# Two-layer mLSTM and convolution trunk: the sums of squares of x issued first, and gated products and gates in another order

## Chip, cores and metric

One Trainium2 chip, one of its cores. The metric is the device time of one launch in microseconds (us). The kernel before took 1609.53 us, the median of three runs (1607.35 to 1611.52).

## What is computed

A trunk of two layers over 512 tokens of 1024 features, all in float32, steered by a vector c. Cut to what matters here:

```python
for l in range(2):
    mod = silu(c) @ w_ada[l] + b_ada[l]            # six rows of 1024: shift, scale, gate, twice
    h = rms_norm(x, g_pre_mix) * (1 + sc_mix) + sh_mix
    x_m, z, glu_a, glu_b = split(h @ w_in[l])      # 4 x 1024 columns
    x_c = silu(causal_conv4(x_m))
    q, k, v = per head of 256: x_c @ w_q, x_c @ w_k, x_m @ w_v
    gates = [q k v] @ w_gates + b_gates            # input and forget gate, 4 heads each
    h_m = sigmoid(z) * head_norm(mlstm(q, k, v, gates))
    a = silu(group_norm(causal_conv31(glu_a * sigmoid(glu_b))))   # 8 groups of 128 channels
    y = concat(h_m, a) @ w_out[l]
    x = x + gt_mix * rms_norm(y, g_post_mix)
    x = x + gt_mlp * rms_norm(relu(h2 @ w_ff1)**2 @ w_ff2, g_post_mlp)   # h2 from x as h above
```

The conv of 31 taps is depthwise: each channel of the gated product has its own 31 weights.

## The kernel before

**Layout.** x lies transposed as eight tiles of 128 features x 512 tokens. A projection of 1024 inputs onto 128 outputs ("a block") is 24 matmuls of 512 columns: weights and h are each split into a high and a low part, and three products are summed (`passes`, L177 to L179). Weights come in by DMA into one of four `raw` buffers; ScalarE rounds the high part (L169), GpSimd, or at the start VectorE, subtracts the low one (L170).

**The mixer.** A string in `ORDERS` (L66) names the order in which the steps of a mixer are emitted. `X i` makes two blocks of x_m, `V i` the conv of four taps with silu, `Q i` q, k and v of head i, the transposes of v (L567) and the head's share of the gates, which VectorE adds up in `gsb` (L578, L583). `G i` makes gated product i out of two blocks (`glu`, L441; VectorE's product is L438). `E` is the gates: two matmuls on `gsb` (L591, L592), a chain of short operations on four partitions that goes between ScalarE and VectorE (L596 to L622) and ends in `mm` (L622), then TensorE's transposes of `al` (L625) and of `mm` (L626) and the tables that VectorE makes of them (L636, L640). `Z i` is a block of the output gate. `N i` is a strip of c's product in layer 0 (L245 to L258). `a i` are the scores of head i: a matmul that spreads `ml` (L647), VectorE's sum (L652), the score products (L660), and VectorE's product (L662), which frees the bank of `mm`-tagged PSUM that L660 filled; there are three such banks. `b`, `c` are the rest of a head, `C i` the 31-tap convs of two groups and their norms, `O` the output projection. The products G0 to G2 are made ahead of the string.

**The convs.** All eight convs of a layer run on VectorE: 31 rows of 128 x 512 a group (the first is L427, the others L429), 248 rows a layer. They are emitted late in the string, with the lowest priority. After each one comes `conv_norm` (L474): ScalarE copies the result (L476), TensorE transposes it (L479), VectorE takes mean and variance (L485, L486, L146) and normalises (L490), TensorE transposes back (L494), VectorE multiplies (L500).

**What sets the order of work.** Each engine has one queue and works through it in order; an instruction that waits holds all that stand behind it. The queues are made before the launch: a list scheduler takes the instructions by priority in a time model of its own and puts conv rows where it reckons that VectorE is free. `behind(later, earlier)` fixes an order of issue, and no wait between engines.

**The start.** DMA issues stand in SyncE's queue. ScalarE and VectorE make silu of c for all partitions (`silu(cbc)`, L210 to L212), then eight squares (L809) and seven sums (L811) of x. TensorE adds over the features (L814), VectorE and GpSimd make the root (L815, L816), TensorE spreads it (L819), and for each tile VectorE and ScalarE make h (L351, L357, L358). TensorE begins with six blocks of layer 0 at once, one tile of h after the other, each with its weights in a `raw` of 384 KB (L168).

Of the kernel before, what the change touches and what calls it, by code (L numbers as in the profile page):

```python
# [10 lines left out]
F32 = mybir.dt.float32  # L11
F32R = mybir.dt.float32r
AF = mybir.ActivationFunctionType
ALU = mybir.AluOpType
PSUM = bass.MemoryType.PSUM

P = 128
T = 512
D = 1024
# [3 lines left out]
NF = D // P  # L23
NC = T // P
KDW = 31
EPS = 1e-6
# [27 lines left out]
def trunk(ctx, tc, xT, vecs, bg, cst, ccol, crow, wadn, wadt, win, win0, wqkv, wgate, wout, wff1, wff2, yT):  # L54
    nc = tc.nc
    pe, dve, act, pool, sp = nc.tensor, nc.vector, nc.scalar, nc.gpsimd, nc.sync
# [3 lines left out]
    wpool = ctx.enter_context(tc.tile_pool(name="wpool", bufs=1))  # L60
    scr = ctx.enter_context(tc.tile_pool(name="scr", bufs=1))
# [1 line left out]
    ps = ctx.enter_context(tc.tile_pool(name="ps", bufs=1, space=PSUM))  # L63

    NSLOT = 25
    ORDERS = ['X0 G3 V0 X1 Q0 V1 N4 G4 X2 G5 N5 Q1 V2 X3 N6 Q2 V3 G6 Q3 E G7 N7 Z0 Z1 Z2 Z3 N8 a0 Z4 b0 Z5 a1 b1 Z6 N9 c0 C0 a2 Z7 c1 b2 C1 C2 C3 O0 O1 a3 O2 c2 O6 O3 b3 O4 O5 c3 O7', 'X0 V0 G3 X1 Q0 V1 X2 G4 Q1 V2 G5 X3 Q2 V3 G7 Q3 E Z0 G6 Z1 Z2 Z3 a0 Z4 Z5 b0 a1 Z6 b1 Z7 c0 a2 c1 C0 b2 C1 C2 C3 O0 O1 a3 O6 O2 c2 O3 b3 O4 O5 c3 O7']  # L66
    WPRI = 300
    NK = 4
    KM = 4
# [4 lines left out]
    RAW = 4  # L74
# [6 lines left out]
    BPRI = 4000  # L81
# [7 lines left out]
    def slot(shape=(P, 2, T), dt=F32):  # L89
        return slots.tile(list(shape), dt, name="slot", tag="slot", bufs=NSLOT)  # L90

    def s2(shape=(P, T), dt=F32):
        return scr.tile(list(shape), dt, name="s2", tag="s2", bufs=S2)
# [4 lines left out]
    def small(n, tag="sm", bufs=16, dt=F32):  # L98
        return sm.tile([P, n], dt, name="small", tag=tag, bufs=bufs)

    def bank(tag, shape=(P, T)):
        n = {"mm": 3, "cv": 2, "ax": 2, "cx": 1}[tag]
        return ps.tile(list(shape), F32, name="ps_" + tag, tag=tag, bufs=n)

    def behind(later, earlier):
        tc.add_manual_dep(later.ins, earlier.ins.name, mybir.DependencyInfo(mybir.DependencyClass.NoSync,
                          mybir.DependencyReason.DATA), reason="order of issue")
# [6 lines left out]
    def r32(ap):  # L114
        return ap.bitcast(F32R)
# [4 lines left out]
    cbc = slots.tile([P, 2, T], F32, name="cbc", tag="slot", bufs=NSLOT).rearrange("p a b -> p (a b)")  # L120
    x = [keep.tile([P, T], F32, name=f"x{i}") for i in range(NF)]
    cc = keep.tile([P, NF], F32, name="cc")
# [10 lines left out]
    ones = cs[:, C_ONE:C_ONE + P]  # L133

    def vec(name, l):
        o, w = VOFF[name]
        return vv[:, l, o:o + w]

    mhalf = keep.tile([P, NC], F32, name="mhalf")
# [10 lines left out]
    def split(pair, src, hi_eng=None, lo_eng=None):  # L150
# [4 lines left out]
            act.copy(out=hi, in_=src)  # L155
        (lo_eng or dve).tensor_tensor(lo, src, pair[:, 0, :], op=ALU.subtract)

    def wblock(src, alloc=None, lo_eng=None, pri=None):
        n = src.shape[-1]
        with tc.high_priority(offset=WPRI if pri is None else pri):  # L160
            flat = lambda t: t.rearrange("p a b -> p (a b)")
            raw = wpool.tile([P, n], F32, name="raw", tag="raw", bufs=RAW)
            if alloc is not None:
                hi, lo = flat(alloc())[:, 0:n], flat(alloc())[:, 0:n]
            else:
                hi = wpool.tile([P, n], F32, name="whi", tag="whi", bufs=WHI)
                lo = wpool.tile([P, n], F32, name="wlo", tag="wlo", bufs=WLO)
            sp.dma_start(out=raw, in_=src)  # L168
            act.copy(out=r32(hi), in_=raw)  # L169
            (lo_eng or pool).tensor_tensor(r32(lo), raw, hi, op=ALU.subtract)  # L170
        return hi, lo

    def passes(out, w, col, pair, first, last, ts=slice(0, T)):
# [9 lines left out]
    def gemm(blocks, pairs):  # L183
        out = bank("mm")
        for b, src in enumerate(blocks):
            spare[0] -= 1
            w = wblock(src, ytile if spare[0] >= 0 else None)
            for k in range(8):
                passes(out, w, k * P, pairs[b * 8 + k], b == 0 and k == 0, b == len(blocks) - 1 and k == 7)
        return out  # L190
# [15 lines left out]
    def half(hf):  # L206
        return slice(hf * (T // 2), (hf + 1) * (T // 2))

    def silu(t, th):
        act.activation(out=th, in_=t, func=AF.Tanh, scale=0.5)  # L210
        act.activation(out=t, in_=t, func=AF.Copy, scale=0.5)
        dve.scalar_tensor_tensor(t, th, 1.0, t, op0=ALU.add, op1=ALU.mult)  # L212

    silu(cbc, wpool.tile([P, D], F32, name="raw", tag="raw", bufs=RAW))
    silu(cc, small(NF))

    hgb = keep.tile([P, L, 24], F32, name="hgb")

# [1 line left out]
    mods = [keep.tile([P, 48], F32, name=f"mod{l}") for l in range(L)]  # L220
    inits = [keep.tile([P, 48], F32, name=f"ini{l}") for l in range(L)]

    def prepare(l):
        for q, (one, gain) in enumerate(ADA):
            k = slice(8 * q, 8 * q + 8)
            if gain is None:
                dve.tensor_copy(out=inits[l][:, k], in_=vec("b_ada", l)[:, k])
            else:
                dve.scalar_tensor_tensor(inits[l][:, k], vec("b_ada", l)[:, k], one, vec(gain, l),
                                         op0=ALU.add, op1=ALU.mult)  # L230

    def ada_rows(nb, tag, alloc=None):

# [28 lines left out]
    def ada_col(l, c, alloc=None):  # L262

        one, gain = ADA[c // 8]
        scale = 1.0 if gain is None else vec(gain, l)[:, c % 8:c % 8 + 1]
        if alloc is not None:
            raw = alloc().rearrange("p a b -> p (a b)")
        else:
            raw = wpool.tile([P, D], F32, name="adr", tag="adr", bufs=ADR)
        sp.dma_start(out=raw, in_=wadt[l, c])  # L270
        m, ini = mods[l][:, c:c + 1], inits[l][:, c:c + 1]
        red = dve.tensor_tensor_reduce(raw, raw, cbc, scale, 0.0 if one else ini, ALU.mult, ALU.add, m)  # L272
        if last[0] is not None:
            behind(red, last[0])
        if one and alloc is not None:
            dve.tensor_tensor(m, m, ini, op=ALU.add)
        elif one:
            late.append((l, c))
# [67 lines left out]
    def make_h(l, i, src, bc, ts, pr, a_off, sh_off, tmp=None):  # L346

        sh = mods[l][:, sh_off + i:sh_off + i + 1]
        hpool = i in HPOOL and ts.stop - ts.start < T
        t = s2() if tmp is None or hpool else tmp(i)  # L350
        dve.scalar_tensor_tensor(t[:, ts], src, mods[l][:, a_off + i:a_off + i + 1], bc, op0=ALU.mult, op1=ALU.mult)  # L351
        if hpool:
            act.activation(out=t[:, ts], in_=t[:, ts], func=AF.Identity, bias=sh)
            act.copy(out=r32(pr[:, 0, ts]), in_=t[:, ts])
            pool.tensor_tensor(r32(pr[:, 1, ts]), t[:, ts], pr[:, 0, ts], op=ALU.subtract)  # L355
            return
        act.activation(out=r32(pr[:, 0, ts]), in_=t[:, ts], func=AF.Identity, bias=sh)  # L357
        dve.scalar_tensor_tensor(r32(pr[:, 1, ts]), t[:, ts], sh, pr[:, 0, ts], op0=ALU.add, op1=ALU.subtract)  # L358

    def finish(l, which, blocks, pairs, y, allocs, nxt):  # L360

# [53 lines left out]
    def mixer(l, hp, pre):  # L415
# [309 lines left out]
        hm = []  # L725
        for step in ORDERS[l].split():
            i = int(step[1:] or 0)
# [74 lines left out]
        return finish(l, "mlp", [wff2[l, 1, m, 1] for m in range(NF)], fp[8:], y, [slot] * KF,  # L802
                      (mix_start(l + 1), [slot] * MK) if l + 1 < L else None)

    prepare(0)
    ss0 = scr.tile([P, T], F32, name="rl", tag="rl", bufs=3)
    for i in range(NF):
        sq = ss0 if i == 0 else scr.tile([P, T], F32, name="rl", tag="rl", bufs=3)
        act.activation(out=sq, in_=x[i], func=AF.Square)  # L809
        if i:  # L810
            dve.tensor_tensor(ss0, ss0, sq, op=ALU.add)  # L811
    v0, u0, r0 = bank("ax"), small(NC), small(NC)
    for c in range(NC):
        pe.matmul(v0[:, c:c + 1], ss0[:, c * P:(c + 1) * P], ones[:, 0:1], start=True, stop=True)  # L814
    dve.tensor_scalar(u0, v0[:, 0:NC], 1.0 / D, EPS, op0=ALU.mult, op1=ALU.add)  # L815
    pool.tensor_tensor(r0, u0, mhalf, op=ALU.pow)  # L816
    bc0 = bank("ax")
    for c in range(NC):
        pe.matmul(bc0[:, c * P:(c + 1) * P], r0[:, c:c + 1].broadcast_to([P, P]), ident, start=True, stop=True)  # L819
    hp, pre = [], {}  # L820
    for j in range(NF // 2):
        if j > 1:
            ada_rows(j, "ax", slot if j == 2 else None)
        for i in (2 * j, 2 * j + 1):
            if j < 2:
                ada_col(0, i, slot)
                ada_col(0, 8 + i, slot)
            pre[i] = wblock(win0[i], slot, dve, 0)
            hp.append(slot())
            make_h(0, i, x[i], bc0, slice(0, T), hp[i], 8, 0)  # L830
    sp.dma_start(out=bgt, in_=bg)
    for l in range(L):
        dve.tensor_scalar(hgb[:, l, 0:8], vec("g_cn", l), 0.5, None, op0=ALU.mult)
        dve.tensor_scalar(hgb[:, l, 8:16], vec("b_cn", l), 0.5, None, op0=ALU.mult)
        dve.tensor_scalar(hgb[:, l, 16:24], vec("b_dw", l), 2.0, None, op0=ALU.mult)
    prepare(1)
    for l in range(L):
        hp, pre = mixer(l, hp, pre)
        hp, pre = mlp(l, hp, pre)
# [61 lines left out]
```

## Time and profile before

| what | value |
|---|---|
| median of three runs | 1609.53 us |
| the profiled execution | 1608.05 us |
| its span, first to last instruction | 1606.3 us |
| busy share of TensorE / VectorE / GpSimd / ScalarE | 96% / 55% / 50% / 43% |
| rows of conv on VectorE | 480 (L429) and 16 (L427) |
| bytes moved | 188.91 MB, mean 118 GB/s |

The program's time is that of the profiled execution, 1.75 us over its span. Busy shares are means over the span; matmuls are pipelined, so a busy TensorE is not one at its peak. The mixer of layer 0 lies between about 70 and 400 us, that of layer 1 between about 860 and 1180 us; between and behind them are the MLPs.

### The profile page before, as it was taken

To read this page: it belongs to the slowest core of one execution; us is meant where nothing else is said; L and a number is where in the kernel's file an instruction comes from. 1 tells how busy PE (TensorE), PEld (TensorE's weight loads), DVE (VectorE), ACT (ScalarE), POOL (GpSimd) and SP (SyncE) were. 2 spreads that over 40 slices of the span, in tenths; PEclk is the share of its full clock that TensorE was granted. 3 is DMA by queue.
4 is the path that set the end of the run, shared out by engine and by line. 5 is a ranking of instruction groups with operands and counts; after the bars stand their busy time and mean duration, and the time that the engine had idled before them with its cause. 6 is when DMAs were issued, how large, how long until landed. Compare 5 with 4: busy or idle time off the path is not lost.

```text
span 1606.3 us, 21229 instructions
## 1 busy us (share of the span) xinstructions
PE 1537.6 (96%) x8020; PEld 1255.5 (78%) x8020; DVE 878.1 (55%) x1761; ACT 688.6 (43%) x1168; POOL 798.5 (50%) x488
## 2 busy tenths in 40 slices
PE   4899998999999999999999999999999999999997
PEld 3577665677998888888899777676899888888887
DVE  6399999843164432346747999997326320012114
ACT  3345563453454322332453665544355432233242
POOL 0166662256744444445962877434674444444462
PEclk9999999999999999999999999999999999999999
DMA  8514332413412555556730222220242233222331
GB/s 309 194 53 138 116 131 104 144 53 92 145 53 94 191 187 197 174 194 218 255 116 8 73 79 67 91 79 27 84 141 65 80 95 102 92 92 92 96 127 53
DMA packets 56270, 188.91 MB, mean 118 GB/s; under 512 B 6376, under 2 KB 8552, under 8 KB 56168
## 3 DMA queue, kind: packets, MB, share of 16 engines
q1 hardware_dynamic: 56168, 187.56, 35.2%
q8 instruction: 63, 1.03, 0.3%
q14 instruction: 39, 0.32, 0.1%
HBM read 185.44 MB, written 2.10 MB: 117 GB/s over the span
## 4 chain that ended last, share of the span: by engine, by line
PE 78%; DVE 6%; ACT 2%; POOL 1%; issue 1%; DMA 0%; POOLq 0%; ACTq 0%; DVEq 0%
PE ps_mm L177 23%; PE ps_mm L179 23%; PE ps_mm L178 23%; DVE ps_cv L429 3%; PE ps_mm L672 2%; PE ps_mm L660 2%; PE ps_ax L316 1%; PE ps_ax L245 1%; POOL wlo L170 1%; ACT whi L169 1%; PE ps_ax L578 1%; PE ps_ax L647 0%; DVE csb L490 0%; PE ps_ax L342 0%; PE ps_ax L701 0%
## 5 line engine op out<-in xcount | busy, mean ns | idle before, releaser
L170 POOL TENSOR_TENSOR wlo<-raw,whi 128x1024 fp32r<-128x1024 f32 (+1 forms) x216 | 498.8, 2311 | 565.1 <-ACT whi L169 547.0
L177 PE MATMUL ps_mm<-slot,whi 128*128 128x512 f32 (+1 forms) x1632 | 621.9, 382 | 8.1 <-ACT slot L155 4.9
L179 PE MATMUL ps_mm<-slot,wlo 128*128 128x512 f32 (+1 forms) x1632 | 622.1, 382 | 5.0 <-POOL wlo L170 4.8
L178 PE MATMUL ps_mm<-slot,whi 128*128 128x512 f32 (+1 forms) x1632 | 621.7, 381 | 0.0
L169 ACT CAST whi<-raw 128x1024 fp32r<-128x1024 f32 (+1 forms) x216 | 216.4, 1002 | 498.9 <-PE ps_mm L178 357.7
L177 PEld LDWEIGHTS ps_mm<-slot,whi 128*128 128x128 f32 x1632 | 307.3, 188 | 78.9 <-ACT slot L155 5.6
L179 PEld LDWEIGHTS ps_mm<-slot,wlo 128*128 128x128 f32 x1632 | 307.6, 188 | 73.8 <-issue 6.3
L178 PEld LDWEIGHTS ps_mm<-slot,whi 128*128 128x128 f32 x1632 | 308.0, 189 | 65.6 <-issue 3.8
L429 DVE SCALAR_TENSOR_TENSOR ps_cv<-slot,vv,ps_cv 128x512 f32<-128x512 f32 x480 | 332.9, 747 | 1.5
L767 DVE TENSOR_TENSOR ps_mm<-rl,ps_mm 128x512 f32<-128x512 f32 (+1 forms) x78 | 46.7, 599 | 280.6 <-ACT rl L766 280.5
L177 PE MATMUL ps_mm<-slot 128*128 128x256 f32 (+1 forms) x568 | 158.5, 292 | 14.5 <-DVE slot L769 7.4
L178 PE MATMUL ps_mm<-slot 128*128 128x256 f32 (+1 forms) x568 | 163.2, 290 | 0.3 <-POOL slot L355 0.3
L179 PE MATMUL ps_mm<-slot 128*128 128x256 f32 (+1 forms) x568 | 162.6, 289 | 0.0
L177 PEld LDWEIGHTS ps_mm<-slot 128*128 128x128 f32 x568 | 105.3, 190 | 19.9 <-ACT slot L357 8.4
L179 PEld LDWEIGHTS ps_mm<-slot 128*128 128x128 f32 x568 | 107.8, 190 | 2.2 <-issue 0.8
L178 PEld LDWEIGHTS ps_mm<-slot 128*128 128x128 f32 x568 | 107.6, 190 | 1.9 <-POOL slot L355 0.5
L170 POOL TENSOR_TENSOR slot<-raw,slot 128x1024 fp32r<-128x1024 f32 x34 | 85.2, 2527 | 14.4 <-issue 12.7
L272 DVE CUSTOM_DVE_ANT_0 adr<-adr,cbc,ini 128x1024 f32<-128x1024 f32 x40 | 66.0, 1659 | 23.3 <-DMA adr<-in_wadt 23.3
L147 POOL TENSOR_TENSOR small<-small,mhalf 128x4 f32<-128x4 f32 (+1 forms) x38 | 34.6, 911 | 81.3 <-DVE small L146 76.6
L769 DVE TENSOR_TENSOR slot<-ps_mm,slot 128x512 fp32r<-128x512 f32 (+1 forms) x78 | 46.4, 595 | 38.2 <-ACT slot L768 37.9
L530 POOL TENSOR_TENSOR xa<-xa,s 128x512 f32<-128x512 f32 x48 | 61.9, 1289 | 5.1 <-ACT s L529 1.9
L768 ACT CAST slot<-ps_mm 128x512 fp32r<-128x512 f32 (+1 forms) x78 | 39.8, 510 | 45.9 <-DVE ps_mm L767 45.9
(201 smaller groups left out, 1570.5 us busy)
## 6 DMA issues: line engine op xcount, KB each, us to landing
raw<-in_wff SPq DMA_DIRECT2D x138, 512.0 KB, 3.5
raw<-in_win SPq DMA_DIRECT2D x58, 512.0 KB, 3.3
adr<-in_wadt SPq DMA_DIRECT2D x56, 512.0 KB, 4.5
raw<-in_wout SPq DMA_DIRECT2D x36, 512.0 KB, 3.5
adr<-in_wadn SPq DMA_DIRECT2D x28, 512.0 KB, 4.2
raw<-in_wqkv SPq DMA_DIRECT2D x24, 256.0 KB, 2.6
slot<-in_wadt SPq DMA_DIRECT2D x8, 512.0 KB, 5.1
raw<-in_win SPq DMA_DIRECT2D x8, 384.0 KB, 7.1
```

Source lines behind the costliest of these rows:

```text
L147: pool.tensor_tensor(y, u, mhalf[:, 0:n], op=ALU.pow)
L169: act.copy(out=r32(hi), in_=raw)
L170: (lo_eng or pool).tensor_tensor(r32(lo), raw, hi, op=ALU.subtract)
L177: pe.matmul(out, whi, xh, start=first, stop=False)
L178: pe.matmul(out, whi, xl, start=False, stop=False)
L179: mark[0] = pe.matmul(out, wlo, xh, start=False, stop=last)
L272: red = dve.tensor_tensor_reduce(raw, raw, cbc, scale, 0.0 if one else ini, ALU.mult, ALU.add, m)
L429: dve.scalar_tensor_tensor(acc, at[i][:, k:k + T], w, acc, op0=ALU.mult, op1=ALU.add)
L530: pool.tensor_tensor(acc, acc, tk, op=ALU.add)
L767: dve.tensor_tensor(o, rl[:, ts], o, op=ALU.mult)
L768: act.copy(out=r32(pr[:, 0, ts]), in_=o)
L769: last[0] = dve.tensor_tensor(r32(pr[:, 1, ts]), o, pr[:, 0, ts], op=ALU.subtract)
```

## The change

Two parts.

1. **Start.** The squares and sums of x, and what makes the root of them, are emitted with a high priority and ahead of silu of c. The squares go into the five buffers of `s2` rather than the three of `rl`. silu(cbc) is placed behind the last sum, the six short copies of `prepare(0)` too, the low part of each tile of h behind the low part of that tile's weights, and `hgb` and `prepare(1)` behind the last tile of h.
2. **Order.** The strings up to the third output gate (the rest is the same but for G6 of layer 1, which moves from behind Z0 to ahead of Q2):

| layer | before | after |
|---|---|---|
| 0 | X0 G3 V0 X1 Q0 V1 N4 G4 X2 G5 N5 Q1 V2 X3 N6 Q2 V3 G6 Q3 E G7 N7 Z0 Z1 Z2 | X0 G3 V0 X1 G4 Q0 V1 N4 X2 G5 Q1 N5 V2 X3 G6 Q2 N6 V3 G7 Q3 Z0 E N7 Z1 Z2 |
| 1 | X0 V0 G3 X1 Q0 V1 X2 G4 Q1 V2 G5 X3 Q2 V3 G7 Q3 E Z0 G6 Z1 Z2 | X0 V0 G3 X1 G4 Q0 V1 X2 G5 Q1 V2 X3 G6 Q2 V3 G7 Q3 Z0 E Z1 Z2 |

```diff
-    def silu(t, th):
-        act.activation(out=th, in_=t, func=AF.Tanh, scale=0.5)
+    def silu(t, th, after=None):
+        first = act.activation(out=th, in_=t, func=AF.Tanh, scale=0.5)
+        if after is not None:
+            behind(first, after)
...
-    prepare(0)
     ss0 = scr.tile([P, T], F32, name="rl", tag="rl", bufs=3)
-    for i in range(NF):
-        sq = ss0 if i == 0 else scr.tile([P, T], F32, name="rl", tag="rl", bufs=3)
-        act.activation(out=sq, in_=x[i], func=AF.Square)
-        if i:
-            dve.tensor_tensor(ss0, ss0, sq, op=ALU.add)
-    v0, u0, r0 = bank("ax"), small(NC), small(NC)
...
+    with tc.high_priority(offset=BPRI):
+        for i in range(NF):
+            sq = ss0 if i == 0 else s2()
+            act.activation(out=sq, in_=x[i], func=AF.Square)
+            if i:
+                laststat = dve.tensor_tensor(ss0, ss0, sq, op=ALU.add)
+        v0, u0, r0 = bank("ax"), small(NC), small(NC)
...
+    silu(cbc, wpool.tile([P, D], F32, name="raw", tag="raw", bufs=RAW), laststat)
+    silu(cc, small(NF))
+    prepare(0, laststat)
...
-            make_h(0, i, x[i], bc0, slice(0, T), hp[i], 8, 0)
+            lasth = make_h(0, i, x[i], bc0, slice(0, T), hp[i], 8, 0)
+            behind(lasth, wlast[0])
```

Lines of the changed kernel lie two to five further down: L429 is L431 there, L583 is L585, L622 is L624, L626 is L628, L660 is L662, L662 is L664.

**SyncE's queue at the start**, before, from the two strips of c's weights (`wadt`) on; `in_win` at 128x768 are the first weights of the GLU blocks, `in_wadn` the strips for `N`:

```order
L270 DMA slot<-in_wadt 128x1024 x2
L168 DMA raw<-in_win 128x768 x4
L241 DMA adr<-in_wadn 128x1024 x3
L831 DMA bgt<-in_bg 4x4
L586 DMA gw<-in_wgate 128x768
L168 DMA raw<-in_win 128x768
```

and now:

```order
L272 DMA slot<-in_wadt 128x1024 x2
L243 DMA adr<-in_wadn 128x1024 x3
L837 DMA bgt<-in_bg 4x4
L588 DMA gw<-in_wgate 128x768
L170 DMA raw<-in_win 128x768 x4
```

Three transfers of 512 KB and one of 384 KB have moved ahead of the first weights. On ScalarE the copy of the first strip of c's product (L248) stood behind a weight's rounding (L169) and now stands ahead of it.

**VectorE in layer 0** around the last share of the gates (L583) and the chain's first operation (L601), before:

```order
L490 TENSOR_SCALAR csb<-ps_cx,small 128x128 x4
L429 SCALAR_TENSOR_TENSOR ps_cv<-slot,vv,ps_cv 128x512 x5
L500 SCALAR_TENSOR_TENSOR yt<-cth,ps_cx 128x512
L429 SCALAR_TENSOR_TENSOR ps_cv<-slot,vv,ps_cv 128x512
L583 TENSOR_TENSOR gsb<-gsb,ps_ax 128x512
L429 SCALAR_TENSOR_TENSOR ps_cv<-slot,vv,ps_cv 128x512 x9
L601 TENSOR_SCALAR s_1652<-s_1649 4x512
```

and now (L585, L603):

```order
L429 TENSOR_SCALAR ps_cv<-slot,vv,hgb 128x512
L431 SCALAR_TENSOR_TENSOR ps_cv<-slot,vv,ps_cv 128x512 x17
L487 BN_STATS small<-ps_cx 128x6 x4
L431 SCALAR_TENSOR_TENSOR ps_cv<-slot,vv,ps_cv 128x512
L488 BN_AGGR small<-small 128x2 x4
L431 SCALAR_TENSOR_TENSOR ps_cv<-slot,vv,ps_cv 128x512
L146 TENSOR_SCALAR small<-small 128x4
L585 TENSOR_TENSOR gsb<-gsb,ps_ax 128x512
L431 SCALAR_TENSOR_TENSOR ps_cv<-slot,vv,ps_cv 128x512 x3
L492 TENSOR_SCALAR csb<-ps_cx,small 128x128 x4
L431 SCALAR_TENSOR_TENSOR ps_cv<-slot,vv,ps_cv 128x512
L603 TENSOR_SCALAR s_1753<-s_1750 4x512
```

Counted from the start of the queue, 184 conv rows stood ahead of the last L583 and 209 ahead of `mm`; now 232 and 248 do, all rows of the layer. Of other operations ahead of `mm` there are four more each of L485, L486 and L490, two more of L500, and one more each of L146 and L438.

**VectorE in layer 1** in the gates' chain, from the second scan (L620) to `mm`, before:

```order
L429 SCALAR_TENSOR_TENSOR ps_cv<-slot,vv,ps_cv 128x512
L619 TENSOR_TENSOR small<-ml,s_8629 4x1
L429 SCALAR_TENSOR_TENSOR ps_cv<-slot,vv,ps_cv 128x512
L620 SCALAR_TENSOR_TENSOR ml<-cs,small,s_8634 4x128
L619 TENSOR_TENSOR small<-ml,s_8629 4x1
L620 SCALAR_TENSOR_TENSOR ml<-cs,small,s_8634 4x128
L619 TENSOR_TENSOR small<-ml,s_8629 4x1
L620 SCALAR_TENSOR_TENSOR ml<-cs,small,s_8634 4x128
L622 TENSOR_TENSOR s_8647<-s_8629,ml 4x512
```

and now (L621, L622, L624):

```order
L621 TENSOR_TENSOR small<-ml,s_8730 4x1
L431 SCALAR_TENSOR_TENSOR ps_cv<-slot,vv,ps_cv 128x512 x2
L622 SCALAR_TENSOR_TENSOR ml<-cs,small,s_8735 4x128
L431 SCALAR_TENSOR_TENSOR ps_cv<-slot,vv,ps_cv 128x512
L502 SCALAR_TENSOR_TENSOR yt<-cth,ps_cx 128x512
L431 SCALAR_TENSOR_TENSOR ps_cv<-slot,vv,ps_cv 128x512
L621 TENSOR_TENSOR small<-ml,s_8730 4x1
L431 SCALAR_TENSOR_TENSOR ps_cv<-slot,vv,ps_cv 128x512 x2
L622 SCALAR_TENSOR_TENSOR ml<-cs,small,s_8735 4x128
L431 SCALAR_TENSOR_TENSOR ps_cv<-slot,vv,ps_cv 128x512 x2
L624 TENSOR_TENSOR s_8748<-s_8730,ml 4x512
```

In layer 1, 186 conv rows stood ahead of `mm` and 202 ahead of the first score product (L662); now 222 and 234 do. On TensorE, in layer 0, 49 matmuls of output gates, four score matmuls (L660) and three groups of four transposes (two of L479, one of L494) that stood behind the first transpose of `mm` (L626) now stand ahead of it, and two of L245 that stood ahead now stand behind. Ahead of the fourth pair of score matmuls of layer 1's first head stands the same work as before.

## Rows read from the trace of the kernel before

**Rows 1.** The page's line of busy time, share of the span and count of instructions by engine.

```profile
PE 1537.6 (96%) x8020; PEld 1255.5 (78%) x8020; DVE 878.1 (55%) x1761; ACT 688.6 (43%) x1168; POOL 798.5 (50%) x488
```

**Rows 2.** Busy time of each engine in stretches of the span: from and to, length, busy us of PE, PEld, DVE, ACT and POOL with instructions, TensorE's granted clock, DMA share and GB/s. The first lies in the start, two in the mixer of layer 0, the last in that of layer 1.

```profile
10.00:15.00 5.00, 0.00 (x0) 0.00 (x0) 4.69 (x23) 2.90 (x5) 0.00 (x0) 1.00 1.03 406
130.00:230.00 100.00, 98.03 (x472) 67.90 (x471) 95.45 (x174) 53.72 (x88) 66.22 (x55) 1.00 0.37 129
84.00:270.00 186.00, 174.79 (x794) 122.84 (x792) 180.03 (x323) 97.74 (x156) 112.25 (x90) 0.97 0.32 111
871.00:1040.00 169.00, 165.39 (x771) 126.70 (x770) 162.64 (x286) 98.38 (x157) 111.29 (x89) 1.00 0.23 74
```

**Rows 3.** The same view in three short stretches in which TensorE's clock fell.

```profile
116.00:122.00 6.00, 6.00 (x19) 4.54 (x20) 6.00 (x10) 3.35 (x7) 5.92 (x6) 0.72 0.09 36
256.00:265.00 9.00, 6.93 (x25) 3.21 (x26) 9.00 (x26) 1.53 (x2) 3.46 (x2) 0.62 0.34 123
1110.00:1118.00 8.00, 6.92 (x20) 4.29 (x20) 6.17 (x23) 3.36 (x9) 2.24 (x2) 0.57 0.00 0
```

**Rows 4.** What TensorE waited for from 76 to 330 us (layer 0): us in total, times, longest.

```profile
PE ps_mm L177 <- ACT slot L155: 4.9, 2, 3.5
PE ps_cx L479 <- ACT csb L476: 2.3, 1, 2.3
PE ps_mm L591 <- DVE gsb L583: 1.9, 1, 1.9
PE ps_ax L625 <- DVE s L612: 1.3, 1, 1.3
```

**Rows 5.** The same from 1040 to 1180 us (layer 1).

```profile
PE ps_mm L660 <- DVE s L662: 1.4, 1, 1.4
PE ps_cx L479 <- DVE yt L500: 0.6, 1, 0.6
PE ps_mm L672 <- DVE s L662: 0.4, 1, 0.4
```

**Rows 6.** VectorE's instructions from 76 to 300 us by line and shape: busy us, mean ns of one, idle time before them and its releaser.

```profile
L429 DVE SCALAR_TENSOR_TENSOR ps_cv<-slot,vv,ps_cv 128x512 f32<-128x512 f32 x227 | 157.0, 746 | 0.6
L490 DVE TENSOR_SCALAR csb<-ps_cx,small 128x128 f32<-128x128 f32 x28 | 9.5, 398 | 0.0
L485 DVE BATCH_NORM_STATS2 small<-ps_cx 128x6 f32<-128x128 f32 x28 | 6.2, 281 | 4.0 <-PE ps_cx L479 4.0
L500 DVE SCALAR_TENSOR_TENSOR yt<-cth,ps_cx 128x512 f32<-128x512 f32 x6 | 4.1, 679 | 2.4 <-ACT ps_cx L498 2.4
L146 DVE TENSOR_SCALAR small<-small 128x4 f32<-128x4 f32 x7 | 3.7, 526 | 0.0
L486 DVE BATCH_NORM_AGGREGATE small<-small 128x2 f32<-128x6 f32 x28 | 2.6, 151 | 0.0
L652 DVE SCALAR_TENSOR_TENSOR s<-ps_ax,cols,cs 128x128 f32<-128x128 f32 x2 | 0.7, 348 | 0.6 <-PE ps_ax L647 0.6
```

**Rows 7.** The timeline of VectorE and of TensorE in layer 0 (first record's start, length, engine, line; two records of TensorE stand for one float32 matmul where its operands are not split).

```profile
269.48 0.67 DVE L622 TENSOR_TENSOR s<-s,ml 4x512 f32<-4x512 f32 x1
...
258.93 3.63 PE L245 MATMUL ps_ax<-adr,cc 128*32 128x512 f32 x12
277.48 0.22 PE L626 MATMUL ps_ax<-cs,s 4*128 4x4 f32 x1
289.96 0.60 PE L479 MATMUL ps_cx<-cs,csb 128*128 128x128 f32 x4
295.37 4.14 PE L660 MATMUL ps_mm<-slot 128*128 128x512 f32 x12
```

**Rows 8.** The same in layer 1; between the last two rows lies one more matmul of the same shape.

```profile
1056.39 0.69 DVE L662 SCALAR_TENSOR_TENSOR s<-ps_mm,s 128x512 f32<-128x512 f32 x1
...
1064.33 0.71 PE L660 MATMUL ps_mm<-slot 128*128 128x128 f32 x4
1065.12 0.39 PE L178 MATMUL ps_mm<-slot,whi 128*128 128x512 f32 x1
...
1065.58 0.39 PE L177 MATMUL ps_mm<-slot,whi 128*128 128x512 f32 x1
```

**Rows 9.** The timeline of the start, engine by engine (VectorE, ScalarE, TensorE, SyncE's issues); in brackets the idle time before and its releaser.

```profile
14.69 0.69 DVE L811 TENSOR_TENSOR rl<-rl 128x512 f32<-128x512 f32 x1
...
16.02 0.83 ACT L169 CAST slot<-raw 128x768 fp32r<-128x768 f32 x1 [2.46 <-DMA raw<-in_win]
22.63 0.72 ACT L357 ACTIVATE slot<-s,mod 128x512 fp32r<-128x512 f32 x1 [5.78 <-DVE s L351]
...
15.43 1.87 PE L814 MATMUL ps_ax<-cs,rl 128*128 128x1 f32 x8 [15.43 <-DVE rl L811]
23.41 1.65 PE L177 MATMUL ps_mm<-slot 128*128 128x512 f32 x3 [1.59 <-ACT slot L357]
...
5.02 1.50 SPq L126 DMA_DIRECT2D x<-in_xT  x3
```

**Rows 10.** The transfers of x: queue, count, size of one, median us from issue to landing.

```profile
x<-in_xT SPq DMA_DIRECT2D x8, 256.0 KB, 5.1
```

**Rows 11.** The timeline of ScalarE, then of TensorE, about the first strip of c's product in the start.

```profile
48.84 1.04 ACT L169 CAST yt<-raw 128x1024 fp32r<-128x1024 f32 x1 [6.03 <-DMA raw<-in_win]
...
50.42 1.05 PE L250 MATMUL ps_ax<-cs,s 128*128 128x1 f32 x8 [1.99 <-ACT s L248]
```

## What was predicted from it

> **What bounds the kernel now.** I read the busy shares first, then the same by stretches, then the waits of the engine that looks fullest, then the queue that it waits for. Over the span TensorE is busy 96% of the time and VectorE 55% [rows 1]: on that view the rest is cover. The stretches say otherwise for the mixers. From 130 to 230 us VectorE is busy 95.45 of 100 us; from 84 us, when the convs run, to 270 us, when `mm` is ready, 180.03 of 186; in layer 1 162.64 of 169 [rows 2]. So ahead of `mm` VectorE has 6.0 us of idle time in layer 0 and 6.4 in layer 1, though TensorE is nearly full too: two engines run level. What TensorE waits for there is short, and most of it comes from the steps that the change moves: 3.5 us at once for the high part of q's input (L155), 1.9 for `gsb`, 2.3 for a conv's copy, 1.3 for `al` [rows 4]. Its clock fell beside them: 0.72 granted from 116 to 122 us, 0.62 from 256 to 265 [rows 3]; both of its levels, 2.4 and 1.2 GHz, lie in those stretches. Where those waits lie the queues decide, and VectorE's slack there is small: it ends `mm` at 270.15 us and TensorE comes for it at 277.48, 7.3 us later [rows 7].
>
> The Trainium skill, on the page Perfetto Trace Analysis (Identifying the Most-Contended Engine), has the engine with the highest occupancy taken as the one to work on, for TensorE by its weight loads; over the span these are 78% here against VectorE's 55% [rows 1], so the rule taken over the span names TensorE, and the change would then be the gain of the first rival below. Taken from 130 to 230 us the same rule names VectorE, 95.45 against 67.90 [rows 2], and the page's next section does say that the engine can change by regime; the trace agrees with this second reading.
>
> **The start: -2.3 us.** Now TensorE first works at 15.43 us, when the last sum is made, and its first real matmul comes at 23.41, behind the high part of h (0.72, L357) [rows 9]. With the squares ahead, the last x sets the sums: its issues end at 6.52 us [rows 9], it lands 5.1 later [rows 10], and a square and a sum cost some 0.7 each, the sum's price [rows 9]: about 13.0 instead of 15.38. The steps behind it are the same, so h could be ready 2.4 earlier, at 21.0. But the weights are late next. They land at 16.0 now, when their rounding starts [rows 9]. Three transfers of 512 KB and one of 384 KB, 1.97 MB, now stand ahead of them; the transfers move 406 GB/s there [rows 2], which is 4.85 us: 20.9. With the rounding (0.83) and h's high part behind it in ScalarE's queue (0.72), the first matmul comes at about 22.4: -1.0. Silu of c goes behind the sums, and the first shift and scale need it: two steps of ScalarE and one of VectorE over 1024 columns, then two reductions as long. By a sum's price for 512 columns, 0.69, each is some 1.4 (an estimate), 13.0 + 5 x 1.4 = 20.0; h could be ready at 21.0 and the weights come at 20.9, which hides it, and `hgb` and the short copies behind it, so I cost them at nothing. Without the late weights silu would be the next to be late, by under 1 us. The second piece: the copy of the first strip (L248) no longer stands behind a rounding that waited 6.03 us for its weight. TensorE waited 1.99 for that copy, and the copy itself takes some 0.6 of the wait [rows 11]: -1.3. Bounds: if the weights land no later, -2.4 and -1.3 are both had, -3.7; if the four first weights land together, another 1.1 MB or 2.9 us later, +0.6.
>
> **Layer 0: +10.0 us.** By the queue, VectorE now has ahead of `mm` 39 more conv rows, four more each of L485, L486 and L490, two of L500, one each of L146 and L438. A conv row costs 157.0 / 227 = 0.69 us, so the rows are 27.0; with 4 x 0.22, 4 x 0.09, 4 x 0.34, 2 x 0.68, 0.53 and 0.68 (L438 has L500's shape) the sum is 32.1 us [rows 6]. All of it lies on VectorE's path, which has no room: 6.0 us of idle time in 186 [rows 2]. Against it stand the slack of 7.3 [rows 7], and the work that TensorE now does before it comes for `mm`: 49 matmuls at 0.23 us (two in 0.46 [rows 8]), 11.3; four score matmuls at 4.14 / 6 = 0.69, 2.8; twelve transposes at 0.15, 1.8; less two of L245 at 0.6 [rows 7], -1.2: 14.7 in all. So TensorE is held 32.1 - 7.3 - 14.7 = 10.1, say 10.0, longer. The waits of now at q and at the gates (9.0 us with those at L479 [rows 4]) are no extra gain: with VectorE the last to be ready, what TensorE wins ahead of `mm` it waits for there. It is not given back afterwards: TensorE's sum of work stays what it was, and what it did early has been counted.
>
> **Layer 1: +9.0 us.** Ahead of the first score product (L662) stand 32 more conv rows, 22.1 us, one more L500, 0.7, and two fewer L652, 0.7 [rows 6]: +22.1. The score matmul that needs this product's bank, the fourth pair, starts at 1064.33, and the product ends at 1057.08 [rows 8]: 7.2 of slack. TensorE's work ahead of that pair is the same as before. So it is held 14.9 longer. Some of that comes back, since later waits are then overtaken: 2.4 us [rows 5], and the clock of 0.57 from 1110 to 1118, which cost 0.43 x 8 = 3.4 [rows 3], as it follows waits that VectorE will no longer cause, all its conv rows being nearly done by then. That leaves +9.1, say 9.0. If the clock falls again elsewhere, 3.4 more.
>
> **Sum.** -2.3 + 10.0 + 9.0 = +16.7 on the profiled execution: 1608.05 to 1624.8. It stands 1.5 below the median, so in terms of the runs 1626. The bounds: with the start at its best (-1.4) and all of VectorE's idle time swallowed by the new conv rows (-6.0 and -6.4 [rows 2]), 1612. Upwards: VectorE's norms wait for TensorE's transposes and ScalarE's copies, 4.0 and 2.4 us in the traced stretch [rows 6], about one us for each of the seven norms; with TensorE itself held up, each of the 14 norms of both layers may wait a us more, +14; with the start at its worst, 1642. I take the middle because nothing in the rows tells which of the two it is nearer to: filling gaps and making new ones are the same queue.
>
> **Rivals.**
>
> *Faster: TensorE stays the bound.* Place: the gates. Z0, 24 matmuls or 5.6 us [rows 8], now lies between the last q and the gates, and G4 covers the wait at the first q. Then the waits of 3.5, 1.9, 2.3 and 1.3 go [rows 4], and the clock's 0.28 x 6 = 1.7 and 0.38 x 9 = 3.4 [rows 3]: -14.1, with the start -16.4, 1593 in terms of the runs. For it: these are TensorE's largest waits, and the steps are moved onto them. Against it: it decides only if VectorE has 32.1 - 7.3 = 24.8 us of room, or conv rows cost 0.1 us less; it has 6.0, and the row's cost is steady.
>
> *No change.* VectorE's idle time goes in both layers, the clock stays high through both, and the start gives its best: about 1612, and up to 1.7 + 3.4 more if the falls of the clock in layer 0 count as gains: 1607. For it: each piece is bounded by a row. Against it: all must hold.
>
> *Worse.* The queues stop each other in turn: norms that wait on TensorE, TensorE that waits on norms and falls to the lower clock at each stop. Each such stop of 2 us with 6 us at half clock behind it costs about 5. Two of them put it over 1642; four at 1647.
>
> *It does not do what it says.* The sums come first on VectorE, and yet the first matmul does not come sooner, since the weights stand behind 1.97 MB. It would take away the start's gain of 1.0 alone, and lies inside the range.
>
> **How the numbers follow.** What a measurement of this kernel can tell from no change is about 0.3%, 4.8 us: 1604.7 to 1614.4. Forecast, by its own bounds 1612 to 1642: 0.70, put above 1614.4 as a whole, since its lowest 2.4 us need all that the case of no change needs. No change 0.10. Faster 0.12. Worse than 1642: 0.08. So faster 0.12, same 0.10, slower 0.78. The range goes from 1606, which takes in nearly all of no change, to 1642; outside lie 0.12 and 0.08.
>
> **What would show it.** VectorE busy over 97% from 84 us until the new `mm` (L624), which ends at about 300 us (270.15 + 32.1 - 2.3); TensorE coming for it (L628) at about 300 too, having waited some 10 us for VectorE on the way; the wait of 3.5 us at L155 gone or smaller; in layer 1 the first score product ending near 1057 + 22 + 8 = 1087. The first matmul at 22.4 and the rounding ahead of it at 20.9. The forecast is wrong if `mm` is done well ahead of TensorE in layer 0, or if VectorE's conv rows come out much under 0.69 us; right in kind and wrong in size, if TensorE's waits on VectorE in the two mixers sum to 5 or to 35 instead of some 20.

## The result

The changed kernel takes 1632.1 us, the median of five runs (1629.88 to 1636.93), against 1609.53: a ratio of 1.0147, interval 1.0132 to 1.0161, slower. The profiled execution took 1636.17 us, with a span of 1634.4; it is one of the two longest of the five, so its rows show some 28 us where the medians show 22.6. Medians and ratios in this document leave out the executions that were disturbed: one of the kernel before (1915.99 us) and the profiled one of the new order in layer 1 alone (3908.77 us), of which no row is read.

The page's line of busy time after, as [rows 1]:

```profile
PE 1542.7 (94%) x8020; PEld 1265.1 (77%) x8020; DVE 875.2 (54%) x1761; ACT 691.3 (42%) x1168; POOL 799.6 (49%) x488
```

TensorE did the same work in a longer span. Where it stood, the busy times by stretch say (columns as in [rows 2]; the second row reaches to the end of `mm`, the last three are TensorE's stops):

```profile
84.00:270.00 186.00, 161.10 (x724) 118.62 (x723) 175.32 (x319) 91.96 (x146) 108.08 (x88) 0.91 0.27 92
84.00:304.00 220.00, 194.59 (x875) 141.19 (x873) 206.62 (x377) 110.02 (x171) 120.86 (x94) 0.92 0.29 97
130.00:230.00 100.00, 87.33 (x409) 63.98 (x408) 93.92 (x176) 50.91 (x82) 56.12 (x46) 0.91 0.30 101
871.00:1040.00 169.00, 168.50 (x866) 137.29 (x866) 153.44 (x271) 90.29 (x152) 108.03 (x91) 1.00 0.21 63
196.00:210.00 14.00, 2.37 (x15) 1.74 (x14) 13.76 (x33) 7.29 (x12) 8.97 (x9) 0.58 0.13 47
243.00:262.00 19.00, 7.74 (x29) 4.06 (x28) 17.21 (x36) 10.51 (x17) 11.22 (x11) 0.67 0.26 97
1076.00:1096.00 20.00, 6.79 (x19) 3.51 (x20) 20.00 (x44) 4.24 (x11) 0.00 (x0) 0.57 0.06 24
```

From 84 to 270 us TensorE is busy 161.10 us instead of 174.79 and VectorE 175.32 instead of 180.03 [rows 2]: both have lost. Two stops in layer 0 and one in layer 1 hold most of it, each with a granted clock near 0.6, so TensorE goes on at its lower level for part of each stretch. In the last VectorE is busy throughout; in the second it has 1.8 us of idle time in 19.

What TensorE waited for from 76 to 330 us, as [rows 4] (L496, L492 and L446 answer to L494, L490 and L444; L446 is ScalarE's tanh of a gated product's gate block, L155 the high part that ScalarE makes of a four-tap conv for a q):

```profile
PE ps_cx L496 <- DVE csb L492: 10.2, 2, 9.1
PE ps_mm L179 <- ACT s L446: 6.1, 3, 2.6
PE ps_mm L179 <- ACT slot L155: 4.3, 1, 4.3
```

and from 1040 to 1180 us, as [rows 5]:

```profile
PE ps_ax L649 <- DVE cols L642: 6.3, 1, 6.3
PE ps_ax L649 <- DVE ml L622: 6.2, 1, 6.2
```

The waits of [rows 4] at `gsb` and at `al` are all but gone; a wait of 9.1 us for one conv's norm (L492) has come, where the longest at that line was 0.2 before. In layer 1 TensorE now waits for the gates' chain itself.

Timeline, as [rows 7] to [rows 9] (VectorE's `mm` in layer 0 and first score product in layer 1; TensorE's first transpose of `mm` and the fourth pair of score matmuls in layer 1; then the start, with the first strip's matmul last):

```profile
303.51 0.68 DVE L624 TENSOR_TENSOR s<-s,ml 4x512 f32<-4x512 f32 x1
1092.73 0.67 DVE L664 SCALAR_TENSOR_TENSOR s<-ps_mm,s 128x512 f32<-128x512 f32 x1
...
305.50 0.22 PE L628 MATMUL ps_ax<-cs,s 4*128 4x4 f32 x1
1093.61 1.22 PE L662 MATMUL ps_mm<-slot 128*128 128x128 f32 x4
...
20.75 0.83 ACT L171 CAST slot<-raw 128x768 fp32r<-128x768 f32 x1 [6.29 <-DMA raw<-in_win]
13.05 1.86 PE L816 MATMUL ps_ax<-cs,rl 128*128 128x1 f32 x8 [13.05 <-DVE rl L813]
22.26 1.65 PE L179 MATMUL ps_mm<-slot 128*128 128x512 f32 x3 [2.54 <-ACT slot L359]
48.09 1.05 PE L252 MATMUL ps_ax<-cs,s 128*128 128x1 f32 x8 [0.71 <-ACT s L250]
```

`mm` is done 34.0 us later than before, TensorE comes for it 28.0 later. The start is as forecast to 0.2 us.

### The profile page after: what moved, and what is told of

Read it like the earlier page. It is cut to its first block, busy times and chain, and to the rows that moved or that the text cites. A ratio compares the mean times of both kernels' runs of the same rounds, so it can differ in the third digit from the quotient of the medians.

```text
span 1634.4 us, 21239 instructions
## 1 busy us (share of the span) xinstructions
PE 1542.7 (94%) x8020; PEld 1265.1 (77%) x8020; DVE 875.2 (54%) x1761; ACT 691.3 (42%) x1168; POOL 799.6 (49%) x488
## 4 chain that ended last, share of the span: by engine, by line
PE 87%; DVE 6%; ACT 3%; DMA 2%; POOL 1%; issue 1%; SPq 0%; POOLq 0%; ACTq 0%; DVEq 0%
PE ps_mm L179 26%; PE ps_mm L180 26%; PE ps_mm L181 26%; DVE ps_cv L431 2%; PE ps_mm L674 2%; PE ps_mm L662 2%; DMA adr<-in_wadn 1%; PE ps_ax L247 1%; PE ps_ax L318 1%; PE ps_ax L580 1%; POOL wlo L172 1%; DMA slot<-in_wadt 0%; DVE slot L274 0%; PE ps_ax L569 0%; PE ps_cx L496 0%
## 5 line engine op out<-in xcount | busy, mean ns | idle before, releaser
L431 DVE SCALAR_TENSOR_TENSOR ps_cv<-slot,vv,ps_cv 128x512 f32<-128x512 f32 x480 | 331.7, 749 | 1.6
L179 PE MATMUL ps_mm<-slot 128*128 128x256 f32 (+1 forms) x568 | 159.6, 295 | 16.7 <-ACT slot L359 10.0
```

The costliest lines, as they stand in the source:

```text
L179: pe.matmul(out, whi, xh, start=first, stop=False)
L431: dve.scalar_tensor_tensor(acc, at[i][:, k:k + T], w, acc, op0=ALU.mult, op1=ALU.add)
```

## The experiments

Each was timed beside the kernel before on the same chip, three chips in all, and ratios are to that; "over the start alone" below divides two such ratios, also across chips. "Mixer 0" and "mixer 1" are lengths in the profiled execution, from VectorE's first record of the layer's first gated product to TensorE's first sum of squares at the mixer's end. "Stood" is TensorE's idle time there, "clock" its busy time multiplied by one minus the granted clock, both summed over rows of 2 us; differences of the two do not add up exactly to a difference in length. All but the kernel before have the new start.

| kernel | ratio | interval | mixer 0 (stood, clock) | mixer 1 (stood, clock) |
|---|---|---|---|---|
| before | 1 | | 359.8 (13.5, 4.6) | 353.4 (6.4, 3.0) |
| the change | 1.0147 | 1.0132 to 1.0161 | 379.6 (28.8, 11.1) | 363.1 (15.9, 5.1) |
| the change again | 1.0149 | 1.0133 to 1.0164 | 378.3 (28.1, 10.7) | 363.4 (15.9, 5.5) |
| start alone | 0.9997 | 0.9986 to 1.0007 | 357.4 (12.4, 1.6) | 355.7 (6.8, 3.1) |
| new order in layer 0 | 1.0124 | 1.0108 to 1.0141 | 376.2 (28.4, 8.1) | 357.6 (7.6, 4.8) |
| new order in layer 1 | 1.0064 | 1.0048 to 1.0081 | no trace | no trace |
| Z0 ahead of E alone | 1.0019 | 1.0008 to 1.0031 | 360.9 (12.9, 4.4) | 357.4 (7.8, 4.6) |
| the change, E ahead of Z0 | 1.0162 | 1.0146 to 1.0178 | 381.3 (30.1, 11.6) | 361.0 (14.1, 4.6) |
| the change, two convs behind mm | 1.0201 | 1.0186 to 1.0215 | 386.7 (34.5, 11.2) | 360.5 (10.1, 6.9) |
| the change, 25 taps | 1.0112 | 1.0096 to 1.0129 | 380.4 (27.4, 12.3) | 351.3 (5.4, 3.2) |
| layer 0 new, strips back | 1.0101 | 1.0084 to 1.0118 | 374.1 (21.8, 12.2) | 358.8 (6.5, 6.5) |
| layer 0 as before, strips moved | 1.0199 | 1.0185 to 1.0213 | 388.5 (34.3, 10.2) | 357.4 (7.1, 6.0) |
| layer 0 as before, G4 early | 0.9981 | 0.9970 to 0.9993 | 354.9 (12.0, 1.5) | 354.4 (6.3, 2.8) |
| layer 1 new, G6 back | 1.0014 | 1.0002 to 1.0026 | 357.4 (12.5, 1.5) | 357.5 (7.4, 4.9) |

A layer that kernels have alike differs by up to 5 us between their traces: layer 1 in the order of before is 353.4 to 358.8 us long, with 2.8 to 6.5 us of clock.

**The parts one by one.** Start alone, with both old strings:

```diff
+ the start as in the change
- X0 G3 V0 X1 G4 Q0 V1 N4 X2 G5 Q1 N5 V2 X3 G6 Q2 N6 V3 G7 Q3 Z0 E N7
+ X0 G3 V0 X1 Q0 V1 N4 G4 X2 G5 N5 Q1 V2 X3 N6 Q2 V3 G6 Q3 E G7 N7 Z0
```

> The new start with the two orders of before. Theory (conv rows ahead of the gates on VectorE make the loss, the start has none): 209 and 186 conv rows ahead of mm as before, first matmul at 22.3 us, the strip's wait down from 2.0 to 0.7 us, so 1.0 to 2.4 us faster than before: 1607 to 1608.5. Rival (the late first weights push the first GLU blocks back, so that the start carries part of the loss): 1612 to 1620.

1609.95 us, a ratio of 0.9997. It carries none of the loss; a gain of 1 to 2 us is inside the interval and is not shown. Its trace is ahead by 4.9 us at the end of mixer 0 and gives it back later, most of it in two stretches at the two ends of the first MLP:

```profile
440.00:500.00 60.00, 56.54 (x464) 55.77 (x463) 34.30 (x94) 33.57 (x81) 25.17 (x19) 0.97 0.21 63
800.00:860.00 60.00, 58.45 (x461) 57.41 (x461) 29.83 (x81) 29.00 (x63) 30.08 (x24) 0.94 0.23 76
```

Both stretches have 1.00 in the kernel before. TensorE is as busy there as it was; 60 x (0.03 + 0.06) = 5.4 us of clock are lost. That alone makes 5 us between two executions.

Behind the gates of layer 0 the clock differs between the orders. From 300 to 320 us, with the start alone (old order):

```profile
300.00:320.00 20.00, 20.00 (x85) 12.56 (x83) 15.10 (x45) 9.33 (x22) 6.29 (x4) 1.00 0.29 106
```

All seven traces with G6 and G7 early in layer 0 have a fall of the clock between 300 and 328 us, worth 1.7 to 8.5 us. The five with G6, G7, Z0 and E in their old places have none there, and Z0 ahead of E alone has one of 3.0 us, from 296 to 304.

Layer 0 alone, layer 1 alone:

> The new start and the new order in layer 0 alone; layer 1 has the order of before. Theory (each layer's loss is its own: 248 conv rows ahead of mm in layer 0, 186 in layer 1): the changed kernel less the 9.5 us that its trace loses after layer 0, so 1632.1 - 9.5 = 1622 to 1624. Rival (the loss of layer 1 follows from what layer 0 left behind): 1632 again.

> The new start and the new order in layer 1 alone. Theory: 209 conv rows ahead of mm in layer 0, 222 in layer 1, so 1609.5 - 1.5 + 9.5 = 1617 to 1619. Rival (the loss of layer 1 follows from layer 0): 1608 as with the start alone.

1630.4 and 1620.6 us (the kernel before: 1610.7 beside them). Both layers lose on their own, so the rivals of both fall. Over the start alone layer 0 costs 1.27%, 20.5 us, more than expected, and layer 1 0.67%, 10.8 us. Their sum, 1.94%, is more than the 1.5% that the change has over the start alone. Why is open; without a trace of layer 1 alone it can't be told whether its run or the change is the odd one.

The gates behind Z0, alone:

```diff
- Q3 E G7 N7 Z0        layer 1: Q3 E Z0 G6
+ Q3 Z0 E G7 N7        layer 1: Q3 Z0 E G6
```

> The new start; of the new orders only that the output gate Z0 stands ahead of the gates E, in both layers (layer 0: Q3 Z0 E G7 N7, layer 1: Q3 Z0 E G6); the gated products stand where they stood before. Theory (what counts is the conv rows ahead of mm, and they are 211 and 186 here): 1607 to 1610, at most 3 us from the start alone. Rival 1 (gates put behind 24 matmuls make the loss): 1620 to 1632. Rival 2 (Z0 covers TensorE's waits at the gates, 1.9 + 2.3 + 1.3 us and the clock's 3.4): 1600.

1614.0 us, 0.22% or 3.5 us over the start alone. Neither rival, and the theory's range is missed by 4 us: the place of the gates is worth little, and it is not a gain. The trace has 2.8 us more of clock in mixer 0 than the start alone.

**Is it VectorE's volume?** The change again, on the chip of the three that follow:

> The changed kernel again, on the chip of the other runs of this call. Theory (layer 0 and layer 1 lose on their own, and the clock's falls spread the runs): 1.3 to 2.0% over before; the sum of the two layers alone was 1.24% and 0.64%. Rival (the two losses share something): 1.2 to 1.5%, well under their sum.

1.0149, as before: inside both ranges, and well under the sum.

The change with E ahead of Z0 again:

> The changed kernel with the gates E ahead of Z0 again in both layers (layer 0: Q3 E N7 Z0 Z1, layer 1: Q3 E Z0 Z1); the gated products stand where the change puts them. Theory (the early gated products let the convs go ahead of the gates): 244 and 216 conv rows ahead of mm against 248 and 222, so 1625 to 1634, within 5 us of the changed kernel. Rival (the place of Z0 makes most of the loss): 1608 to 1616.

1637.3 us, above the range but within 1.2 us of the change beside it (1636.1). What costs is in the places of G and of the strips.

Two of the eight convs moved behind `mm`:

```diff
+    LATE = 6
...
                    if k == 0:
-                        dve.tensor_scalar(acc, at[i][:, 0:T], w, hgb[:, l, 16 + i:17 + i], op0=ALU.mult, op1=ALU.add)
+                        first = dve.tensor_scalar(acc, at[i][:, 0:T], w, hgb[:, l, 16 + i:17 + i], op0=ALU.mult, op1=ALU.add)
+                        if i >= LATE:
+                            behind(first, mmi[0])
...
-            dve.tensor_tensor(mm, bl, ml, op=ALU.add)
+            mmi[0] = dve.tensor_tensor(mm, bl, ml, op=ALU.add)
```

> The changed kernel, but the first conv row of groups 6 and 7 is put behind mm in VectorE's queue, in both layers. Nothing else is changed, the steps stand in the new order. 186 conv rows stand ahead of mm in each layer instead of 248 and 222 (before: 209 and 186). Theory (VectorE's rows ahead of mm are the loss): the loss goes, 1600 to 1612. Rival 1 (TensorE's queue in the new order has the stops in it, at the norms' second transposes and at c's strips): 1622 to 1634. Rival 2 (the convs are now late at the other end, where the output projection needs them): 1615 to 1630, with TensorE waiting for conv rows behind 330 us.

1643.3 us, above all three ranges. The theory falls for layer 0: with 62 conv rows fewer ahead of `mm`, mixer 0 is 7 us longer still. TensorE's queue is not quite the same, as the scheduler makes it anew (12 records stand inside the sixth norm instead of 3). Two stretches, then the waits from 240 to 262 us (lines lie up to four further down: L156 is L155, L500 and L496 are L496 and L492):

```profile
240.00:260.00 20.00, 8.54 (x36) 5.17 (x34) 4.16 (x16) 8.16 (x13) 9.95 (x9) 0.70 0.34 127
260.00:280.00 20.00, 17.69 (x77) 12.80 (x77) 1.63 (x3) 9.53 (x15) 8.60 (x7) 0.87 0.25 79
```

TensorE stands for 11.5 of 20 us while VectorE is busy 4.16. The second stop of layer 0 needs no busy VectorE. Rival 1 has the place right, not the size. Rival 2 has little: behind 330 us TensorE's waits on VectorE in mixer 0 are 1.8 us. Mixer 1 gains 2 to 3 us where its loss was some 7, and has new waits of 2.1 and 1.7 us for the norms that are now late.

```profile
PE ps_mm L180 <- ACT slot L156: 4.5, 1, 4.5
PE ps_cx L500 <- DVE csb L496: 3.3, 1, 3.3
```

TensorE waits for the high part that ScalarE makes of a four-tap conv, and for a norm.

25 of 31 taps:

```diff
-            for k in range(KDW):
+            for k in range(25):
```

> The changed kernel with 25 of the 31 taps of the convs; the last six taps are left out in both layers. Each layer has 48 conv rows fewer, 33 us of VectorE, and 200 stand ahead of mm in each. Theory (VectorE's volume ahead of the gates is what holds TensorE): 1595 to 1612, the level of the kernel before or under it. Rival (the order of the steps, whatever VectorE has to do): 1622 or more.

1629.5 us: the theory is missed and the rival's range met, and the run parts the layers: mixer 1 is at 351.3 us, shorter than before, mixer 0 at 380.4, as long as in the change. Layer 1 is VectorE's volume; layer 0 has something that stays when that volume goes.

**The new theory for layer 0.** What fills TensorE's queue while VectorE is at a norm? In the timeline of the change, about the stop of 9.1 us, without the rows of the split matmuls (which end before L252 and come again behind L496):

```profile
195.68 0.95 PE L252 MATMUL ps_ax<-cs,s 128*128 128x1 f32 x8
196.49 0.63 PE L481 MATMUL ps_cx<-cs,csb 128*128 128x128 f32 x4
206.20 1.12 PE L496 MATMUL ps_cx<-cs,csb 128*128 128x128 f32 x4 [9.08 <-DVE csb L492]
```

and the same norm in the kernel before:

```profile
202.55 0.60 PE L479 MATMUL ps_cx<-cs,csb 128*128 128x128 f32 x4
...
221.02 0.60 PE L494 MATMUL ps_cx<-cs,csb 128*128 128x128 f32 x4
```

A norm takes VectorE 9 us or more, conv rows and GpSimd's root included. Before, 76 rows of TensorE's queue lie between the transposes out and back; now none, and 3 in the sixth norm of the layer (before 33). The strips are the part that does it, by the order of the queue: with N5 and N6 behind Q1 and Q2, the products of q, k and v are spent when the strip and the four-tap conv come.

The whole new order of layer 0 with the strips where they were:

```diff
- X2 G5 Q1 N5 V2 X3 G6 Q2 N6 V3 G7
+ X2 G5 N5 Q1 V2 X3 G6 N6 Q2 V3 G7
```

> The new start and, in layer 0, the new order but with the strips N5 and N6 ahead of Q1 and Q2 as they were before (G5 N5 Q1 V2 X3 G6 N6 Q2 V3 G7 Q3 Z0 E N7); layer 1 has the order of before. In TensorE's queue 46 and 47 rows now stand between a norm's transposes out and back where the new order has 0 and 3 (before: 76 and 33), and 244 conv rows stand ahead of mm (new order 248, before 209). Theory formed after the last call (the strips between q and the conv of four taps leave TensorE's queue with nothing between those transposes, so that it stands through VectorE's norm twice, about 9 us each with what follows at half clock): the loss of layer 0 goes for the most part, 1610 to 1619. Rival, the prediction's (conv rows ahead of mm): 1624 to 1632, as with the whole new order of layer 0 (1630.4).

1625.7 us, 1.04% or 16.7 us over the start alone: inside the rival's range, and the theory's is missed. Against the whole new order of layer 0 (1.0124) the strips' old place wins 0.23%, and the two intervals overlap. The bare norms are gone, and TensorE's standing that is left is mostly the prediction's mechanism, VectorE's queue ahead of the gates:

```profile
240.00:260.00 20.00, 10.42 (x40) 7.91 (x39) 20.00 (x39) 7.28 (x11) 5.53 (x4) 0.66 0.09 27
300.00:320.00 20.00, 19.90 (x59) 10.84 (x60) 7.57 (x35) 5.66 (x17) 1.01 (x1) 0.57 0.32 107
```

VectorE is busy 20.00 of 20 us and TensorE half of them. In mixer 0 TensorE stands 9.4 us longer than with the start alone, which the prediction had at 10, and has 10.6 us more of clock; against the trace of the kernel before it is 8.3 and 7.6. The second row holds 8.5 us of that clock, with hardly any idle time: it is the fall behind the gates. TensorE has gone over there to small matmuls: strips (L247), spreads from four partitions (L649), sums into one column (L252). Whether they or the stops before them bring the clock down was not tested. Its waits, and rows of the timeline in that fall:

```profile
PE ps_cx L481 <- ACT csb L478: 9.6, 1, 9.6
PE ps_mm L593 <- DVE gsb L585: 3.8, 1, 3.8
PE ps_cx L496 <- DVE csb L492: 3.8, 1, 3.8
...
300.59 3.05 PE L247 MATMUL ps_ax<-adr,cc 128*32 128x512 f32 x12
303.57 2.07 PE L649 MATMUL ps_ax<-ml,cs 4*128 4x512 f32 x2
308.47 1.71 PE L252 MATMUL ps_ax<-cs,s 128*128 128x1 f32 x8
```

The first two are waits for conv rows: ScalarE's copy (L478) waits for the last row of a conv. The third is still a norm's, with 15 records inside it.

The old order of layer 0 with the strips moved, and nothing else:

```diff
- G5 N5 Q1 V2 X3 N6 Q2 V3 G6
+ G5 Q1 N5 V2 X3 Q2 N6 V3 G6
```

> The new start and, in layer 0, the order of before but with N5 and N6 behind Q1 and Q2 (Q1 N5 V2 X3 Q2 N6 V3); the gated products and the gates stand where they stood, and layer 1 has the order of before. 3 and 4 rows of TensorE's queue stand between a norm's transposes out and back in two places, and 217 conv rows ahead of mm (before 209). Theory (the strips' place): 1620 to 1632, with two stops of TensorE between 190 and 265 us. Rival (conv rows): 8 rows or 5.5 us more against a slack of 7.3, so 1608 to 1614.

1641.5 us, 2.02% or 32 us over the start alone, above the theory's range, with 8 more conv rows ahead of `mm`. From 180 to 320 us TensorE waits for:

```profile
PE ps_mm L179 <- ACT slot L155: 12.9, 3, 4.7
PE ps_cx L496 <- DVE csb L492: 6.2, 2, 3.4
PE ps_mm L179 <- ACT s L446: 4.8, 1, 4.8
```

The place of two strips alone costs more than the whole change. More of the waiting is for the four-tap convs beside the norms (L155, 12.9 us) than for the norms (6.2). The two causes don't add, 16.7 and 32 against 20.5 together. The early G4, G6 and G7 may fill part of what the strips lay bare; that was not tested, nor a kernel with the strips back and fewer conv rows.

G4 alone, ahead of the first Q:

```diff
- X1 Q0 V1 N4 G4 X2
+ X1 G4 Q0 V1 N4 X2
```

> The new start and, in layer 0, G4 ahead of the first Q instead of behind N4, nothing else of the new orders. 207 conv rows ahead of mm, at least 32 rows of TensorE's queue inside each of the first six norms. Theory (the good half of the change: a block of a gated product covers the wait of 3.5 us for the first q's input and keeps the clock up there, 1.7 us): 1603 to 1607. Rival (VectorE runs level with TensorE, so TensorE waits for it later): 1608 to 1612, as with the start alone (1609.95).

1605.5 us, 0.9981, interval 0.9970 to 0.9993: faster than both kernels. From 116 to 122 us, where [rows 3] have a clock of 0.72:

```profile
116.00:122.00 6.00, 6.00 (x27) 4.84 (x26) 5.97 (x10) 3.95 (x7) 5.09 (x7) 1.00 0.25 89
```

The wait of 3.5 us at L155 for the first q is gone, with 1.0 us at L446 in its place. Over the start alone (0.9997, and 0.91 in that stretch) the intervals overlap: start and G4 together are a gain, and G4's own share, 2.5 us of mixer 0 in the traces, is not clear of the noise.

Layer 1 in the new order with G6 behind the gates:

```diff
- X3 G6 Q2 V3 G7 Q3 Z0 E Z1
+ X3 Q2 V3 G7 Q3 Z0 E G6 Z1
```

> The new start, layer 0 in the order of before, and layer 1 in the new order but with G6 behind Z0 and E as before (Q2 V3 G7 Q3 Z0 E G6 Z1). 225 - 209 less: 434 conv rows in all ahead of mm of layer 1 as before, where the new order has 470, so 186 of the layer instead of 222. Theory (in layer 1 conv rows ahead of the gates' chain make the loss, and the early G6 is what lets them go there): 1608 to 1613. Rival (the early G4 and G5, or Z0 ahead of the gates): 1617 to 1621, as with the whole new order of layer 1 (1620.9).

1611.3 us, 0.17% over the start alone where the whole new order of layer 1 has 0.67%. In the stretch of the stop of layer 1:

```profile
1076.00:1096.00 20.00, 19.04 (x80) 14.42 (x79) 20.00 (x45) 8.35 (x21) 5.73 (x3) 1.00 0.12 38
```

VectorE is full here too, and TensorE works beside it. Most of layer 1's loss is the early G6, whose conv rows stand ahead of the gates' chain.

## Where the prediction held and where it failed

- **Direction and place**: right. Two mixers lose and the start does not; 1626 was forecast, 1632.1 came, inside the range.
- **The start**: right in each step (sums at 13.05 us, forecast 13.0; rounding at 20.75, forecast 20.9; first matmul at 22.26, forecast 22.4; the strip's wait 0.7 instead of 2.0). The 2.3 us that it was forecast to be worth could not be shown: the interval of the start alone reaches from -2.3 to +1.1 us.
- **Layer 0, +10.0**: the step that failed, in its size. It is +19.8 in the trace and 20.5 timed on its own. The term priced TensorE's standing and put the clock at nothing. With the strips back 16.7 us are left: 9.4 of standing, near the 10.0 (3.8 of it a norm's wait, which the term did not count), and 10.6 of clock, most of it behind the gates and not beside a wait. And the sum gave the strips' new place no price, though it leaves TensorE's queue bare for two norms and the four-tap convs beside them. That costs 32 us alone, and on top of the early products 3.7, which is not clear of the noise: in the change the strips settle where TensorE stops more than for how long.
- **VectorE full until `mm`**: wrong. It is busy 206.62 of 220 us from 84 us to the end of `mm`, 94% where over 97 was forecast, and from 84 to 270 us its idle time grew from 6.0 to 10.7 us; the stops held it as well. `mm` came at 304.2 us and TensorE at 305.5, about 300 forecast. The wait at the first q went, and one of 4.3 us at L155 came later, at 253 us.
- **Layer 1, +9.0**: right in cause and nearly in size, the size in part by luck. It is +9.7 in the trace (7.4 over the start alone; 4.3 to 9.7 over the traces with the old order), 10.8 timed on its own. The fourth pair of score matmuls starts 0.2 us behind the first score product, as forecast, but some 10 us later in the mixer where 14.9 were forecast; and of the 5.8 us that were to come back next to nothing did, the clock costing 2.1 more instead of 3.4 less. The two misses cancel. The first score product ends at 1093.4 us, 6 later than forecast: layer 0 brings 11 more than forecast, layer 1 itself 5 less. 25 taps takes the loss away and G6's place most of it.
- **The sign for a wrong size**: TensorE's waits on VectorE in the two mixers sum to 25 us, 11.4 and 13.6, where some 20 were forecast, so this sign did not show that layer 0 was mis-sized; it does not count the clock.
- **The rivals**: "TensorE stays the bound" had a gain at the first q, of which the traces of the G4 experiment show about half, and the gates' cover wrong: Z0 ahead of E costs 3.5 us. "Worse", norms that TensorE waits on and a lower clock at its stops, is nearest to what layer 0 did, at a smaller size than its 1642. By its own price of 5 us a stop, two stops make 1636 and not over 1642; it takes four.

The Trainium skill's Perfetto Trace Analysis (Optimization Strategy) says to look within a regime for the gaps and what blocks there. The traces agree: in layer 1's stop VectorE is busy 20.00 of 20 us, and its queue is what blocks. In layer 0 the gap of 9.1 us named a norm, and only a count of TensorE's queue, 0 rows where 76 had been, said why it was bare.

## What to carry to other kernels

Where an in-order engine sends work out and takes it back (a norm's transposes here), count in the new queue what stands between the two; a step that is only moved can be the one that covered it. Beside the volume on the engine that is level with the bound, give TensorE's lower clock a price: here, over the start alone, 0.2 to 1.1 us went with each us of standing. Time a change of order piece by piece, and also take each piece out of the whole: here two steps cost 32 us alone and 3.7 in the whole, and a gain of 0.2% (start and G4) lay under a loss of 1.5%.

## What was not expected of the hardware

TensorE's lower clock does not only stand beside a stop. With the strips back its stops lie between 235 and 271 us; from 280 to 300 it is busy 19.34 of 20 us at 1.00, and from 300 to 320 it is busy 19.90 of 20 at a granted clock of 0.57. A fall there comes back in all seven traces with G6 and G7 early, so it goes with the order. Other falls do not: at the MLP's end two executions with nearly the same waits (1.0 and 1.5 us) had 1.00 and 0.94 over 60 us. So a comparison of two traces has 3 to 5 us of clock in it that the kernels' order does not explain.
